# Cosine and sine tables of a state-space stage: two stored copies, or one copy that each load reads twice

## The chip, the core and the metric

The kernel runs on one core of a Trainium2 chip. The metric is the time of one execution on the device in microseconds (us); the kernel before was timed three times. One execution was also recorded by the hardware profiler, and all durations below are from that one.

## The reference, cut to what matters

Two layers work on 512 tokens of width 1024: chunked gated linear attention (GLA), then an S5 layer, each with an input projection, a gated branch of width 2048 and an output projection. The change is in the S5 layer. It runs 128 groups of 16 channels, each with 64 complex states:

```
lam_bar = jnp.exp(lam * dt)
bu = lax.complex(einsum(u, real(b_bar)), einsum(u, imag(b_bar)))
_, states = lax.associative_scan(combine, (a, bu), axis=1)      # state <- lam_bar * state + bu
y = einsum(real(states), c_re) - einsum(imag(states), c_im)
y = gelu(y + d_skip * u);  y = y * sigmoid(y @ w_glu + b_glu) * silu(z)
return y @ w_out
```

## The kernel before, in words

**Dense work.** All projections are products of 128x512 blocks on TensorE (PE). Weights come from HBM in units of 512 KB (`wunit`, L175, into one of two `wraw` buffers), and are split into a high and a low part on ScalarE (ACT, L158 or L180) and VectorE (DVE, L159) or by an accumulating DMA from GpSimd (POOL), into one of eight `whl` buffers. Each product is three matmuls (L189 to L195).

**The S5 recurrence.** The sequence is cut in 64 chunks of 8 tokens. Inside a chunk the recurrence is a small product; between chunks it is a scan on DVE with a real decay, which needs the states turned by an angle that depends on state, group and chunk before the scan and turned back after it. The turning uses tables of cosine and sine: for each of the 16 blocks (`cb`) of 8 groups, 512 values of each for each of the 64 states. Since real and imaginary parts of the states lie on partitions 0 to 63 and 64 to 127, the loaded table has to stand on both halves.

**Where the tables come from and go.** While the GLA layer runs, the class `S5Prep` prepares the S5 constants on DVE and stores them to scratch tensors in HBM: `bmd`, `cmd`, `gmd`, and the tables in `tab`. `etab(ck)` computes two blocks at once, on partitions 0 to 63 and 64 to 127 (six DVE instructions, L1251 to L1256), and stores each twice, to rows 0 to 63 and to rows 64 to 127 of its block (L1257 to L1260). Later `load_a(cb)` and `load_b(cb)` bring a block's four constants back through `loadw`: the first three blocks as two halves into `big` buffers (L569), the other 13 as one load of 512 KB into `q4` buffers (L572; the profile shows them as `q`). `sA` uses them: L795 to L798 are the first turn.

**What sets the order.** A scheduler with its own timing model orders the instructions of each engine when the kernel is built; `issue_after` and priorities steer it. Nearly all loads and stores are issued by SyncE (SP), in one order; an SP instruction that waits holds up those behind it. The `q4` tag has nine buffers, which the preparation, the blocks' constants and the gate outputs share, so that a load for a later block waits until an earlier block has been used. `F` steps of the preparation (L1267 to L1273) load `lpt` and `s_bi`, both with written-out patterns: `lpt` is read as 16 copies (step 0) of 8 rows, `s_bi` as 16 rows of 8 copies.

Of the kernel before, what the change touches and what calls it, by code (L numbers as in the profile page):

```python
# [9 lines left out]
F32 = mybir.dt.float32  # L10
# [11 lines left out]
P = 128  # L22
# [8 lines left out]
NS = 64  # L31
T = 8
NC = SEQ // T
GB = 8
NB = 16
# [52 lines left out]
def trunk_kernel(  # L88
# [5 lines left out]
    nc = tc.nc  # L94
# [3 lines left out]
    dr = ctx.enter_context(tc.tile_pool(name="dr", bufs=1, space=DRAM))  # L98
    cnt = [0]

    def T_(shape, tag, bufs, dt=F32):
        cnt[0] += 1
        return sb.tile(shape, dt, tag=tag, name=f"{tag}_{cnt[0]}", bufs=bufs)

    def C_(shape, name, dt=F32):
        return sb.tile(shape, dt, tag=name, name=name, bufs=1)
# [17 lines left out]
    def q4(dt=F32, n=1024):  # L124
        return T_([P, n], "q4", Q4, dt)
# [7 lines left out]
    def xx(dt=F32):  # L133
        return T_([P, 512], "xx", 8, dt)
# [189 lines left out]
    prep = S5Prep(tc, dr, C_, T_, PT, ident, q4, q2, big, tmp, s_bi, s_xc)  # L324
# [143 lines left out]
    for i in range(2):  # L468
        a = C_([P, P], f"att{i}")
# [87 lines left out]
    def loadw(cb, src, dt=F16):  # L557
        n = 1024 if dt == F16 else 512
        if src is prep.gmd:
            srcs = [src[cb, 4 * k:4 * k + 4].rearrange("g p w -> p g w") for k in range(2)]  # L560
            full = src[cb].rearrange("g p w -> p g w")
        else:
            srcs = [src[cb][:, k * n:(k + 1) * n] for k in range(2)]
            full = src[cb]
        fit = (lambda t: t.rearrange("p (g w) -> p g w", w=2 * P)) if src is prep.gmd else (lambda t: t)
        if cb < NPRE:
            w = [T_([P, n], "big", BIG, dt) for _ in range(2)]
            for k in range(2):
                S.dma_start(out=fit(w[k]), in_=srcs[k])  # L569
            return w  # L570
        t = q4(dt, 2 * n)
        S.dma_start(out=fit(t), in_=full)  # L572
        return [t[:, :n], t[:, n:]]
# [8 lines left out]
    def load_a(cb):  # L582
        t = st_[cb]
        t["bm"] = wsel(loadw(cb, prep.bmd))
        t["cs"] = loadw(cb, prep.tab, F32)

    def load_b(cb):
        t = st_[cb]
        t["gh"] = gsel(loadw(cb, prep.gmd))
        t["cm"] = wsel(loadw(cb, prep.cmd))  # L590
# [37 lines left out]
    for h in range(NH):  # L628
        v = ([], [])
        box = []  # L630
        o = ([], [])
# [64 lines left out]
    for i in range(2):  # L696
        r = xx().rearrange("p (g c) -> p g c", g=GB)
# [207 lines left out]
    for tb in range(NT):  # L905
        for k in range(2):
            S.dma_start(out=f(x1p)[k * 64:(k + 1) * 64, 2 * tb:2 * tb + 2].rearrange("p q d -> p (q d)"),
                        in_=x1d.rearrange("(c j) d -> j c d", j=T)[2 * tb + k])
# [21 lines left out]
class S5Prep:  # L930
    def __init__(self, tc, dr, C_, T_, PT, ident, q4, q2, big, tmp, s_bi, s_xc):
        self.tc = tc
        self.nc = nc = tc.nc
        self.C_, self.T_, self.PT, self.ident = C_, T_, PT, ident
        self.q4, self.q2, self.big, self.tmp = q4, q2, big, tmp
        self.s_bi, self.s_xc = s_bi, s_xc
        self.kz = dr.tile([NG, 16, KW * 2], F16, name="kz")
        self.bmd = dr.tile([NB, P, 2 * GB * P], F16, name="bmd")
        self.cmd = dr.tile([NB, P, 2 * GB * P], F16, name="cmd")
        self.gmd = dr.tile([NB, GB, P, 2 * P], F16, name="gmd")  # L940
        self.tab = dr.tile([NB, P, 2 * GB * NC], F32, name="tab")
        self.pw = dr.tile([2 * NS, NG, 2 * T], F32, name="pw")
        self.lpt = dr.tile([T, NG, 2, NS], F32, name="lpt")
        self.bcd = dr.tile([2, NS, NG], F32, name="bcd")
        self.r8d = dr.tile([NS, NG], F32, name="r8d")
        self.kdd = dr.tile([NG, 16], F32, name="kdd")
        self.etd = dr.tile([NG], F32, name="etd")
        self.t = 0
        self.ld = {}
        self.res = {}  # L950
# [290 lines left out]
    def etab(self, ck):  # L1241
        nc = self.nc
        tt = nc.vector.tensor_tensor
        gs = slice(ck * GB, (ck + 1) * GB)
        hr, hi, lr, li = (t[:, gs] for t in self.et)
        shp = [P, GB, 8, 8]
        up = lambda t: t.unsqueeze(3).to_broadcast(shp)
        dn = lambda t: t.unsqueeze(2).to_broadcast(shp)
        e = self.q4().rearrange("p (r g a b) -> p r g a b", r=2, g=GB, a=8)
        u = self.tmp().rearrange("p (g a b) -> p g a b", g=GB, a=8)  # L1250
        tt(out=e[:, 0], in0=up(hr), in1=dn(lr), op=MUL)  # L1251
        tt(out=u, in0=up(hi), in1=dn(li), op=MUL)
        tt(out=e[:, 0], in0=e[:, 0], in1=u, op=SUB)
        tt(out=e[:, 1], in0=up(hr), in1=dn(li), op=MUL)
        tt(out=u, in0=up(hi), in1=dn(lr), op=MUL)
        tt(out=e[:, 1], in0=e[:, 1], in1=u, op=ADD)  # L1256
        for k in range(2):  # L1257
            for r in range(2):
                nc.sync.dma_start(out=self.tab[k * 8 + ck, r * 64:(r + 1) * 64],
                                  in_=e[k * 64:(k + 1) * 64].rearrange("p r g a b -> p (r g a b)"))  # L1260

    def load(self, cb):
        S = self.nc.sync
# [155 lines left out]
```

## Time and profile before

| what | value |
|---|---|
| runs shown | 1040.68, 1044.32, 1048.78 us; median 1044.32 |
| profiled execution | 1042.2 us, of which the recorded span is 1040.5 us |
| mean granted clock of TensorE | 0.943 of full speed |
| busy share of the span | PE 89%, DVE 69%, ACT 45%, POOL 10% |
| moved by DMA | 205.79 MB; HBM read 167.69 MB, written 45.59 MB |

PE, DVE, ACT and POOL are the compute engines; SP only issues transfers. The page of the profile cuts the span into 40 slices and gives for each the busy tenths of an engine, the granted clock of PE and the mean busy share of the core's 16 DMA engines. Other views group instructions by line, list who waited for whom, list transfers with the time from issue to landing, or give the sums over a chosen stretch of the span.

### The profile page before, as it was taken

To read this page: it belongs to the slowest core of one execution; us is meant where nothing else is said; L and a number is where in the kernel's file an instruction comes from. 1 tells how busy PE (TensorE), PEld (TensorE's weight loads), DVE (VectorE), ACT (ScalarE), POOL (GpSimd) and SP (SyncE) were. 2 spreads that over 40 slices of the span, in tenths; PEclk is the share of its full clock that TensorE was granted. 3 is DMA by queue.
4 is the path that set the end of the run, shared out by engine and by line. 5 is a ranking of instruction groups with operands and counts; after the bars stand their busy time and mean duration, and the time that the engine had idled before them with its cause. 6 is when DMAs were issued, how large, how long until landed. Compare 5 with 4: busy or idle time off the path is not lost. (4 is left out here: it accounts for less than half of the span.)

```text
span 1040.5 us, 13590 instructions
## 1 busy us (share of the span) xinstructions
PE 921.3 (89%) x5019; PEld 715.9 (69%) x5019; DVE 715.5 (69%) x1225; ACT 471.4 (45%) x707; POOL 101.2 (10%) x168
## 2 busy tenths in 40 slices
PE   6895961899969984989999979999999999999996
PEld 5573750676747763767777768787778888888885
DVE  5793559977899768988947758798998542424322
ACT  5553342436546643543666573743443532313212
POOL 4175700002001200000100000000000000000000
PEclk9997985799979987999999989999999999999998
DMA  8884376899979999899684526777766432252312
GB/s 258 233 180 99 69 203 196 233 263 286 295 229 246 287 284 288 235 281 312 214 247 171 182 92 218 249 263 254 237 186 200 128 102 83 99 170 93 101 61 81
DMA packets 118707, 205.79 MB, mean 198 GB/s; under 512 B 32400, under 2 KB 69824, under 8 KB 118640
## 3 DMA queue, kind: packets, MB, share of 16 engines
q1 hardware_dynamic: 110208, 180.90, 54.9%
q0 software_dynamic: 5472, 19.02, 9.9%
q10 hardware_dynamic: 2960, 4.99, 1.4%
q8 instruction: 39, 0.64, 0.2%
q14 instruction: 28, 0.23, 0.1%
HBM read 167.69 MB, written 45.59 MB: 205 GB/s over the span
## 5 line engine op out<-in xcount | busy, mean ns | idle before, releaser
L159 DVE TENSOR_TENSOR whl<-wraw,whl 128x1024 fp32r<-128x1024 f32 x100 | 122.0, 1222 | 156.5 <-ACT whl L158 156.2
L158 ACT CAST whl<-wraw 128x1024 fp32r<-128x1024 f32 x100 | 104.9, 1049 | 191.1 <-PE pd L194 50.2
L193 PE MATMUL pd<-whl,actA 128*128 128x512 f32 x384 | 152.9, 404 | 13.3 <-ACT whl L158 9.0
L194 PE MATMUL pd<-whl,actA 128*128 128x512 f32 x384 | 153.0, 398 | 0.0
L195 PE MATMUL pd<-whl,actA 128*128 128x512 f32 x384 | 151.4, 399 | 0.0
L189 PE MATMUL pd<-actA,whl 128*128 128x512 f32 x256 | 102.3, 406 | 7.3 <-ACT u L723 6.2
L191 PE MATMUL pd<-actA,whl 128*128 128x512 f32 x256 | 101.4, 397 | 0.0
L193 PEld LDWEIGHTS pd<-whl,actA 128*128 128x128 f32 x384 | 73.1, 191 | 32.4 <-ACT whl L158 9.0
L195 PEld LDWEIGHTS pd<-whl,actA 128*128 128x128 f32 x384 | 72.9, 190 | 17.6 <-issue 2.4
L194 PEld LDWEIGHTS pd<-whl,actA 128*128 128x128 f32 x384 | 73.1, 190 | 16.9 <-issue 1.2
L193 PE MATMUL pd<-whl,q 128*128 128x512 f32 x192 | 79.0, 412 | 4.4 <-DVE tmp L387 2.7
L194 PE MATMUL pd<-whl,q 128*128 128x512 f32 x192 | 77.9, 406 | 0.0
L180 ACT CAST whl<-wraw 128x1024 fp32r<-128x1024 f32 x36 | 37.7, 1047 | 74.7 <-PE pd L194 32.2
L189 PEld LDWEIGHTS pd<-actA,whl 128*128 128x128 f32 x256 | 48.6, 190 | 19.8 <-ACT u L723 7.2
L191 PEld LDWEIGHTS pd<-actA,whl 128*128 128x128 f32 x256 | 48.7, 190 | 11.3
L189 PE MATMUL po<-actA,whl 128*128 128x512 f32 x128 | 51.7, 404 | 3.8 <-ACT whl L180 3.8
L190 PE MATMUL pd<-actA,whl 128*128 128x512 f32 x128 | 52.1, 407 | 0.0
L191 PE MATMUL po<-actA,whl 128*128 128x512 f32 x128 | 50.4, 396 | 1.3 <-DMA whl<-w_qk 1.3
L195 PE MATMUL pd<-whl,q 128*128 128x512 f32 x128 | 50.9, 409 | 0.0
L723 ACT ACTIVATE u<-pd,rsP 64x256 f32<-64x256 f32 x64 | 48.2, 753 | 3.5 <-DVE mxr L716 2.6
L190 PE MATMUL pd<-big,whl 128*128 128x512 f32 x120 | 47.6, 398 | 1.1 <-DVE big L159 1.1
L193 PEld LDWEIGHTS pd<-whl,q 128*128 128x128 f32 x192 | 37.3, 194 | 15.4 <-DVE tmp L387 3.1
(327 smaller groups left out, 2001.2 us busy)
## 6 DMA issues: line engine op xcount, KB each, us to landing
wraw<-w_glu SPq DMA_DIRECT2D x32, 512.0 KB, 3.5
wraw<-w_v SPq DMA_DIRECT2D x16, 512.0 KB, 4.7
wraw<-w_z SPq DMA_DIRECT2D x16, 512.0 KB, 6.7
whl<-w_z POOLq DMA_DIRECT2D x16, 512.0 KB, 7.9
q<-lpt SPq DMA_DIRECT2D x16, 512.0 KB, 6.8
q<-s_bi SPq DMA_DIRECT2D x16, 512.0 KB, 8.5
wraw<-w_out SPq DMA_DIRECT2D x16, 512.0 KB, 5.5
bmd<-q SPq DMA_DIRECT2D x16, 512.0 KB, 5.1
```

The costliest lines, as they stand in the source:

```text
L158: i0 = A.copy(out=dst_hi, in_=src)
L159: i1 = V.tensor_tensor(out=dst_lo, in0=src, in1=f(dst_hi), op=SUB)
L180: A.copy(out=hi, in_=raw)
L189: PE.matmul(acc, lhsT=wh, rhs=ah, start=first, stop=False)
L190: PE.matmul(acc, lhsT=wh, rhs=al, start=False, stop=False)
L191: mark["pe"] = PE.matmul(acc, lhsT=wl, rhs=ah, start=False, stop=last).ins
L193: PE.matmul(acc, lhsT=ah, rhs=wh, start=first, stop=False)
L194: PE.matmul(acc, lhsT=ah, rhs=wl, start=False, stop=False)
L195: mark["pe"] = PE.matmul(acc, lhsT=al, rhs=wh, start=False, stop=last).ins
L723: A.activation(out=dst, in_=src, func=AF.Copy, scale=rsP[hs, tb:tb + 1])
```

## The change

`tab` gets 64 rows for each block in place of 128. `etab` stores each block once: two stores of 256 KB for a call in place of four, so 16 in the program in place of 32. `loadw` reads the 64 rows twice, by a pattern whose first count is 2 with step 0, then 64 rows, then the run of the row. The tile that a load fills, and its size, stay as they are.

```diff
+        if src is prep.tab:
+            w2 = 2 * GB * NC
+            both = lambda o, m: bass.AP(src.tensor, src[cb].offset + o, [[0, 2], [w2, NS], [1, m]])
+            srcs, full = [both(k * n, n) for k in range(2)], both(0, w2)
         fit = (lambda t: t.rearrange("p (g w) -> p g w", w=2 * P)) if src is prep.gmd else (lambda t: t)
...
-        self.tab = dr.tile([NB, P, 2 * GB * NC], F32, name="tab")
+        self.tab = dr.tile([NB, NS, 2 * GB * NC], F32, name="tab")
...
         for k in range(2):
-            for r in range(2):
-                nc.sync.dma_start(out=self.tab[k * 8 + ck, r * 64:(r + 1) * 64],
-                                  in_=e[k * 64:(k + 1) * 64].rearrange("p r g a b -> p (r g a b)"))
+            nc.sync.dma_start(out=self.tab[k * 8 + ck], in_=e[k * 64:(k + 1) * 64].rearrange("p r g a b -> p (r g a b)"))
```

The scheduler places everything anew. The first place is SP's queue at the first two calls of `etab`; each row is an instruction with its target, its source and its size. Before:

```order
L1259 DMA tab<-q_232_1282 64x1024 x4
L1272 DMA big_1408<-s_xc 128x512
L1259 DMA tab<-q_241_1343 64x1024 x2
L1273 DMA pp_1409<-pw 128x128
L1259 DMA tab<-q_241_1343 64x1024 x2
L1309 DMA cmd<-q_261_1451 128x2048
L1309 DMA bmd<-q_305_1646 128x2048
L1267 DMA q_311_1665<-lpt 128x1x1024
```

In the changed program, whose lines behind `loadw` are numbered 4 and behind `etab` 2 higher:

```order
L1262 DMA tab<-q_232_1282 64x1024 x2
L1274 DMA big_1404<-s_xc 128x512
L1262 DMA tab<-q_241_1341 64x1024 x2
L1311 DMA cmd<-q_261_1447 128x2048
L1275 DMA pp_1405<-pw 128x128
L1311 DMA bmd<-q_305_1640 128x2048
L1269 DMA q_311_1659<-lpt 128x1x1024
```

Four of eight stores are gone, and `cmd` stands one place ahead of `pp`. The second place is SP's queue where the third block's halves are loaded, at the end of the GLA layer. In the changed program:

```order
L175 DMA wraw_4130<-w_out 128x1024
L175 DMA wraw_4170<-w_out 128x1024
L573 DMA big_4209<-bmd 128x1024
L573 DMA big_4210<-bmd 128x1024
L1342 DMA gmd<-kz 1024x1x256
L573 DMA big_4213<-tab 128x1x512
L1337 DMA kz<-kf_3738 128x256
L573 DMA big_4214<-tab 128x1x512
L573 DMA big_4217<-gmd 128x4x256
L175 DMA wraw_4296<-s_wu 128x1024
```

Before, the copy `gmd<-kz` stood between the two `tab` halves instead of ahead of both, and their rows read `tab 128x512`. The third place is the main S5 stage; in the changed program:

```order
L576 DMA q_1017_5252<-bmd 128x2048
L576 DMA q_1018_5254<-tab 128x1x1024
L576 DMA q_1019_5256<-gmd 128x8x256
L576 DMA q_1020_5258<-cmd 128x2048
L175 DMA wraw_5267<-s_wz 128x1024
```

From here on SP's order is the same as before, load by load. Only the form of the `tab` row differs, `128x1x1024` for `128x1024`: the source now has counts of its own (2, 64, 1024), as the `lpt` row of the first place has.

## Rows read from the trace of the kernel before

**Rows 1.** The page: busy us of each engine, and its DMA row.

```profile
PE 921.3 (89%) x5019; PEld 715.9 (69%) x5019; DVE 715.5 (69%) x1225; ACT 471.4 (45%) x707; POOL 101.2 (10%) x168
DMA  8884376899979999899684526777766432252312
```

**Rows 2.** Stretches: start:end, us, busy us by engine, granted clock, DMA share, GB/s.

```profile
176.00:220.00 44.00, 35.03 (x139) 26.63 (x138) 41.05 (x71) 20.89 (x32) 2.63 (x3) 0.79 0.85 232
300.00:400.00 100.00, 95.84 (x414) 73.86 (x410) 82.33 (x142) 54.55 (x80) 10.67 (x11) 0.95 1.00 280
400.00:420.00 20.00, 6.50 (x31) 3.85 (x31) 17.62 (x40) 9.82 (x18) 1.73 (x2) 0.57 0.92 249
456.00:480.00 24.00, 21.29 (x85) 14.95 (x84) 22.47 (x48) 8.66 (x18) 1.03 (x1) 0.93 0.98 325
480.00:510.00 30.00, 28.45 (x135) 21.28 (x133) 25.69 (x46) 14.82 (x30) 0.00 (x0) 1.00 0.66 226
543.00:630.00 87.00, 78.81 (x646) 62.45 (x646) 56.21 (x92) 55.49 (x74) 0.34 (x2) 0.96 0.46 152
630.00:752.00 122.00, 119.83 (x1079) 95.95 (x1078) 106.95 (x154) 58.39 (x83) 1.90 (x11) 1.00 0.75 249
```

**Rows 3.** DMA issues: count, KB of each, median us from issue to landing.

```profile
q<-lpt SPq DMA_DIRECT2D x16, 512.0 KB, 6.8
q<-s_bi SPq DMA_DIRECT2D x16, 512.0 KB, 8.5
...
wraw<-s_wu SPq DMA_DIRECT2D x16, 512.0 KB, 3.5
...
q<-tab SPq DMA_DIRECT2D x13, 512.0 KB, 6.5
```

**Rows 4.** SP's time for one issue, ns minimum/median/maximum, by line.

```profile
L1259 SPq DMA_DIRECT2D tab<-q x32: 452/654/1544, 177.7 to 539.0; - x32
L572 SPq DMA_DIRECT2D q<-tab x13: 319/383/660, 543.3 to 752.5; - x13
L1267 SPq DMA_DIRECT2D q<-lpt x16: 520/530/1324, 144.9 to 440.5; - x16
```

**Rows 5.** Waits that DVE (300 to 400 us) and PE (400 to 500 us) ended.

```profile
DVE q L1283 <- DMA q<-s_bi: 10.3, 3, 4.7
...
PE pt L1323 <- DVE q L162: 7.5, 1, 7.5
PE pt L1323 <- DVE big L159: 5.7, 1, 5.7
```

**Rows 6.** SP in order of time: start, us, line.

```profile
363.75 2.77 SPq L1259 DMA_DIRECT2D tab<-q  x4
...
474.81 0.55 SPq L1340 DMA_DIRECT2D gmd<-kz  x1
...
481.10 0.33 SPq L175 DMA_DIRECT2D wraw<-s_wu  x1
```

**Rows 7.** ACT in order of time: the split of the first `s_wu` unit.

```profile
494.62 1.05 ACT L158 CAST whl<-wraw 128x1024 fp32r<-128x1024 f32 x1 [3.62 <-PE pd L194]
```

**Rows 8.** DMA from 630 to 752 us: GB/s in 40 slices, then `tab` loads.

```profile
GB/s 305 363 259 364 208 0 198 336 361 309 103 335 380 167 60 0 174 361 409 334 105 216 363 374 248 115 340 357 365 39 156 349 376 316 15 0 244 258 330 348
...
q<-tab SPq DMA_DIRECT2D x9, 512.0 KB, 6.5
```

**Rows 9.** SP in order of time: two `tab` loads of that stretch.

```profile
647.86 0.32 SPq L572 DMA_DIRECT2D q<-tab  x1
...
665.67 0.51 SPq L572 DMA_DIRECT2D q<-tab  x1
```

**Rows 10.** DVE: the first uses of these two tables.

```profile
667.22 0.69 DVE L795 TENSOR_TENSOR tmp<-po,q 64x512 f32<-64x512 f32 x1
...
701.39 0.69 DVE L795 TENSOR_TENSOR tmp<-po,q 64x512 f32<-64x512 f32 x1
```

**Rows 11.** Waits of SP's queue, 540 to 770 us.

```profile
SPq L572 <- PE pt L765: 54.2, 13, 9.9
```

## The prediction

> **What bounds the kernel now.** I read the page first [rows 1]. PE is busy 921.3 of 1040.5 us, and no other engine is near it, so a gain can come only where PE waits, or where something that it needs comes late. The DMA row has digits of 8 and 9 in its first fifteen and then around slice 19, and 5 to 7 afterwards: transfers are a near-bound in the GLA layer, where the preparation runs, and have room later. Then I took stretches [rows 2]. The reader is to see three things there. From 300 to 400 us the 16 DMA engines are full (share 1.00, 280 GB/s) while PE still gets 95.8 of 100 us. From 400 to 420 us PE works only 6.5 of 20 us, and its granted clock falls to 0.57. And from 630 to 752 us PE is full (119.8 of 122 us) with a DMA share of 0.75. The waits [rows 5] say why PE stands at 400: its small matmuls of the preparation (L1323) wait 7.5 and 5.7 us for DVE, which shortly before had waited 10.3 us for the `s_bi` loads. So transfers are paid for there by way of DVE, and behind 630 us they are hidden, as long as they come in time.
>
> **The stores.** Sixteen of 32 stores of 256 KB go. On SP each takes a median of 0.654 us [rows 4], 10.5 us in all; SP is no compute engine, and what counts is what it issues behind them. Half belong to the first four calls of `etab`, of which the first starts at 177.7 us [rows 4] and the fourth at 363.75 [rows 6]; the other half belong to the last four, the last of them at 539.0 [rows 4]. A call saves 0.5 MB, or 1.9 us of full DMA at the 280 GB/s of 300 to 400 us [rows 2]. Two of these calls lie in the full stretch and two ahead of it, where DVE is the busiest (41.05 of 44 us from 176 to 220) and the DMA share is 0.85. The last four lie where PE loses little (28.45 of 30 us busy from 480 to 510), so I count them as nothing; their cover is PE's own work, and without it they save another 7.5. The gain lies between 0 and 4 x 1.9 = 7.5 us; I take 3, since only part of DVE's waiting reaches PE.
>
> **The order.** Some matmuls of the preparation change places by a few rows, `cmd` goes ahead of `pp`, and `gmd<-kz` goes ahead of a `tab` load. Nothing is added to an engine. What this costs isn't in the trace; it can go either way, and the nearest row is the 13.2 us of stall that PE has behind L1323 [rows 5], as a whole given back or had once more. I take 0, and keep 5 us on each side, because the rows that move stay within a few places.
>
> **The loads, issue.** A load of `tab` becomes a source with written-out counts, like `lpt`, whose issue takes 0.530 us against 0.383 [rows 4]: 19 loads, 2.8 us of SP. In the S5 stage SP waits 54.2 us for buffers that PE has still to free [rows 11], which covers it; without that cover it is 2.8 us.
>
> **The loads, on the engines.** This is the term that decides. Before, a load is 128 rows, spread evenly over 16 engines: 8 rows each. Now its pattern is 2 x 64 rows, with steps of 0 and 1024 elements, which don't merge into one count. How such a pattern is spread isn't shown by any row. At one end it is spread as before, at no cost. At the other, the first count decides, and two engines carry 64 rows each. The nearest rows are `lpt` and `s_bi` [rows 3], the other loads with two counts: they land in 6.8 and 8.5 us, near the 6.5 of the flat load, but their first count is 16, so both readings fit them. What is new is the 2, and I take the end at which it counts: a flat 128, or a 16 in front, is what all large loads here have in common. I further take it that it is the same two engines each time.
>
> [...]
>
> *From 630 to 752 us.* A share of 0.75 at 249 GB/s [rows 2] is 249 / 0.75 / 16 = 20.75 GB/s for a busy engine, or 0.197 us for a row of 4 KB; the fastest slice, 409 GB/s [rows 8], is 25.6 GB/s, or 0.160 us. An engine is busy 0.75 x 122 = 91.5 us. Nine `tab` loads [rows 8] are 72 rows of that, 14.2 us (11.5 at the fast price), and other transfers 77.3 (80.0). With 64 rows a load, two engines get 576 rows, 113.5 (92.2) us, together 190.8 (172.2) us in a stretch of 122: 69 (50) us too much. Every other load has a share on these two engines and lands no sooner than they do, weights included. What absorbs some of it is the lead of the loads. Two of them [rows 9] are first used 19.4 and 35.7 us after their issue [rows 10]; less the 6.5 us of landing, 12.9 and 29.2, on average 21. That leaves 48 (29) us; I take 38. The bounds are 0, if leads grow by themselves, and 69. From 543 to 630 us three loads add 3 x 56 x 0.197 = 33 us to 0.46 x 87 = 40 us, which fits into 87: nothing there.
>
> *From 456 to 510 us.* Six loads of 256 KB, rows of 2 KB: two engines get 336 rows or 688 KB more, 33 us at 20.75 GB/s, 27 at 25.6, in a stretch with a share of 0.98 [rows 2]. From 480 to 510 us 0.34 x 30 = 10.2 us are free for it. Queued behind are the store of `kz` and the copy `gmd<-kz` that waits for it at 474.81 us, and behind that in SP's order the first `s_wu` unit at 481.10 [rows 6]. That unit lands after 3.5 us [rows 3] and is split at 494.62 [rows 7], so it has 10 us to spare. 27 to 33, less 10.2, less 10, are 7 to 13 us of PE standing; I take 10, with bounds of 0 and 33.
>
> **The sum.** -3 + 0 + 0 + 38 + 10 = +45 us on the profiled execution of 1042.2 us. The median of the runs is 1044.3, 2.1 above, so I predict 1089 us. With the longer lead, the fast price, no loss before 510 us and the full gain of the stores it is 50 - 29 - 7.5 = +13.5, or 1058; with the shorter lead, the slow price and the full 33 us it is 69 - 13 + 33 = +89, or 1133. That is the range of this case.
>
> **Rivals.**
> *Sixteen engines as before.* The two counts are spread over all engines. For it speaks that `lpt` and `s_bi`, with two counts, pay nothing; against it that theirs begin with 16. Then only the stores are left: 1044.3 - 3 = 1041 us, not slower. It decides at the stall at 400 us, behind the third and fourth call: to be faster by over 1%, most of its 13.2 us [rows 5] have to go, where two stores' worth of DMA is 1.9 us a call. It shows by `tab` loads that still land in under 8.5 us.
> *Two engines, but other ones each time.* Then each load takes 64 x 0.160 to 0.197 = 10 to 13 us in place of 6.5, within the smallest lead of 12.9 beyond landing, and no engine is full for long: 1041 to 1050, say 1044. Against it: nothing in the trace shows a rotation.
> *Two engines, and no lead helps.* The loads of the next block start only when PE has freed buffers [rows 11], so a late load delays the next one's start, and PE's clock falls in its pauses, as at 400 us [rows 2]: up to 1044.3 + 69 + 33 = 1146, say 1140.
>
> **Chances.** A measurement of this kernel tells about 1%, 10 us, from no change. The forecast gets 0.70, since no other large load has a first count that leaves engines out and the excess of 50 to 69 us is twice the lead; 0.04 of it ends within 1%, the rest slower. Sixteen engines get 0.17, of which 0.05 faster and 0.12 the same; rotation 0.08, of which 0.07 the same and 0.01 slower; no lead 0.05, slower. Together: faster 0.05, same 0.23, slower 0.72. The range of 1040 to 1132 leaves out half of the sixteen-engine case (0.085), the last rival (0.05) and the forecast's upper tail (some 0.05).
>
> **What would show it.** Right: the median landing of `q<-tab` rises above 10 us; the DMA share falls while the S5 stage grows; waits of DVE's L795 for `q<-tab`, and of ACT's L158 for `wraw`, appear; PE's idle time grows behind 456 us and hardly before. HBM written falls by 4.2 MB in any case. Wrong: `q<-tab` lands in 5 to 8 us (sixteen engines), or in 10 to 13 us with PE as full as before (rotation); or PE loses its time ahead of 456 us, which would be the order.

## The result, and the profile after

The changed kernel takes 1132.7 us (median of 4 runs, 1128.1 to 1135.7) against 1043.0 us for the kernel before (four runs), a ratio of 1.085 with an interval of 1.082 to 1.089. The profiled execution took 1128.1 us (span 1126.4) against 1042.2, so 85.9 us have to be found. The numbers of lines behind `loadw` are four higher in the changed kernel (L576 for L572, L836 for L832).

The page of the changed kernel, PE's busy row, the DMA row by slices and the first part of the chain of waits [rows 1]:

```profile
PE 945.8 (84%) x5019; PEld 730.8 (65%) x5019; DVE 714.8 (63%) x1225; ACT 470.0 (42%) x707; POOL 99.8 (9%) x168
...
DMA  8864466999789988648645356464566432244222
...
PE 46%; DMA 25%; DVE 15%; ACT 6%; issue 4%; SPq 2%; POOL 0%; ACTq 0%; DVEq 0%; POOLq 0%
```

PE runs the same 5019 matmuls in 24.5 us more, and stands the other 61 us. The DMA digits go down in the middle of the program, not up, though what is loaded is the same. The same stretches as in [rows 2]:

```profile
300.00:400.00 100.00, 96.10 (x399) 72.47 (x400) 81.71 (x141) 51.12 (x76) 10.69 (x11) 0.96 0.96 265
...
456.00:480.00 24.00, 18.67 (x74) 13.90 (x73) 22.01 (x42) 7.15 (x11) 1.03 (x1) 0.86 0.61 210
480.00:510.00 30.00, 21.23 (x68) 15.05 (x68) 14.02 (x28) 7.17 (x16) 0.00 (x0) 0.72 0.51 166
630.00:752.00 122.00, 101.57 (x825) 80.98 (x826) 70.22 (x106) 54.99 (x78) 1.03 (x6) 0.89 0.49 152
```

From 300 to 400 us nothing has changed that matters. From 456 us on PE's busy time falls, its granted clock with it (1.00 to 0.72 from 480 to 510 us), and the DMA share drops from 0.98 to 0.61 and from 0.75 to 0.49. Engines that stand while others have a queue would look like this.

Fixed times compare different work, so I cut both traces at the same loads: the first, the seventh (the first of 512 KB), the tenth and the last `tab` load. Before, these were issued at 455.88, 543.30, 629.88 and 752.45 us; after, at 461.41, 564.43, 659.14 and 836.09. Columns as in [rows 2]; first the kernel before:

```profile
455.88:543.30 87.42, 81.67 (x379) 61.93 (x378) 68.98 (x129) 43.93 (x78) 4.06 (x7) 0.98 0.81 261
543.30:629.88 86.58, 78.39 (x643) 62.08 (x642) 55.95 (x91) 55.20 (x74) 0.34 (x2) 0.96 0.46 152
629.88:752.45 122.57, 120.16 (x1080) 96.16 (x1080) 107.51 (x154) 58.84 (x84) 1.90 (x11) 1.00 0.75 249
```

and the changed kernel:

```profile
461.41:564.43 103.02, 86.15 (x373) 65.15 (x372) 67.54 (x127) 43.20 (x77) 4.06 (x7) 0.88 0.62 202
564.43:659.14 94.71, 79.57 (x643) 63.20 (x642) 56.13 (x91) 55.06 (x74) 0.34 (x2) 0.91 0.45 138
659.14:836.09 176.95, 130.99 (x1080) 103.70 (x1080) 107.02 (x153) 56.81 (x82) 1.89 (x11) 0.87 0.58 176
```

Ahead of the first load the program is 5.5 us later. The three stretches grow by 15.6, 8.1 and 54.4 us, and what follows by 2.3: together 85.9. In the last stretch the matmuls are the same 1080; 43.6 of the 54.4 us are PE standing, and 10.8 are the same matmuls at a granted clock of 0.87 in place of 1.00.

The medians from issue to landing [rows 3]; the table loads have none in this trace:

```profile
wraw<-s_wz SPq DMA_DIRECT2D x16, 512.0 KB, 14.8
...
q<-gmd SPq DMA_DIRECT2D x13, 512.0 KB, 10.9
...
xx<-yd SPq DMA_DIRECT2D x16, 256.0 KB, 8.0
```

Weights of `s_wz` landed in 5.9 us before, `gmd` in 6.5, `xx<-yd` (y coming back through HBM) in 4.2. What is late is the flat loads beside the table loads. SP's time for one issue, ns minimum/median/maximum, as in [rows 4]:

```profile
L576 SPq DMA_DIRECT2D q<-tab x13: 512/512/781, 564.4 to 836.1; - x13
L576 SPq DMA_DIRECT2D q<-gmd x13: 370/436/10653, 577.1 to 860.9; - x13
L576 SPq DMA_DIRECT2D q<-cmd x13: 319/1817/10721, 581.7 to 862.4; - x13
```

Before, the longest issue of these lines was 2.8 us (`cmd`). Now SP is held for up to 10.7 us in a single issue. One round in the S5 stage, from the timeline of the changed kernel (start, duration, engine; in brackets the idle time before and what ended it), shows how that reaches PE:

```profile
676.50 0.38 SPq L175 DMA_DIRECT2D wraw<-s_wz  x1
677.11 0.51 SPq L576 DMA_DIRECT2D q<-tab  x1
677.67 1.08 SPq L831 DMA_DIRECT2D xx<-yd  x1
679.19 10.65 SPq L576 DMA_DIRECT2D q<-gmd  x1
689.93 4.25 SPq L576 DMA_DIRECT2D q<-cmd  x1
...
695.49 0.72 ACT L836 ACTIVATE big<-xx,mx 128x512 f32<-128x512 f32 x1 [10.72 <-DMA xx<-yd]
699.71 1.04 ACT L158 CAST whl<-wraw 128x1024 fp32r<-128x1024 f32 x1 [3.50 <-DMA wraw<-s_wz]
700.66 2.91 ACT L727 ACTIVATE u<-pd,rsP 64x256 f32<-64x256 f32 x4
...
703.62 0.79 PE L189 MATMUL pd<-actA,whl 128*128 128x512 f32 x1 [10.47 <-ACT u L727]
```

The load of `xx` leaves SP half a microsecond behind a table load. ACT gets its data 18 us later, and its evictions of `u` are queued behind that, and PE stands 10.5 us for `u`. Before, from 543 us to 24 us behind the last `tab` load (776 us), ACT waited 3.3 us for `xx<-yd` and 10.4 for `s_wz`; in the changed kernel, over the same work (543 to 860 us):

```profile
ACT whl L158 <- DMA wraw<-s_wz: 56.4, 7, 14.9
ACT big L836 <- DMA xx<-yd: 23.4, 7, 10.7
```

### The profile page after: what moved, and what is told of

Same layout as the page of the kernel before. It is cut to its first block, busy times and chain, and to the rows that moved or that the text cites. A ratio compares the mean times of both kernels' runs of the same rounds, so it can differ in the third digit from the quotient of the medians.

```text
span 1126.4 us, 13569 instructions
## 1 busy us (share of the span) xinstructions
PE 945.8 (84%) x5019; PEld 730.8 (65%) x5019; DVE 714.8 (63%) x1225; ACT 470.0 (42%) x707; POOL 99.8 (9%) x168
## 4 chain that ended last, share of the span: by engine, by line
PE 46%; DMA 25%; DVE 15%; ACT 6%; issue 4%; SPq 2%; POOL 0%; ACTq 0%; DVEq 0%; POOLq 0%
DMA wraw<-s_wz 7%; PE pd L193 6%; PE pd L194 6%; PE pd L195 6%; DMA big<-s_xc 4%; PE pd L190 4%; PE pd L189 4%; PE pd L191 4%; ACT u L727 3%; DMA wraw<-w_v 2%; DMA q<-s_bi 2%; DVE whl L159 2%; PE po L189 2%; PE po L190 2%; PE po L191 2%
## 5 line engine op out<-in xcount | busy, mean ns | idle before, releaser
L189 PE MATMUL pd<-actA,whl 128*128 128x512 f32 x256 | 107.2, 426 | 40.1 <-ACT u L727 20.8
L191 PE MATMUL pd<-actA,whl 128*128 128x512 f32 x256 | 105.3, 412 | 0.0
L193 PE MATMUL pd<-whl,q 128*128 128x512 f32 x192 | 81.3, 425 | 18.1 <-DVE tmp L387 8.2
L189 PEld LDWEIGHTS pd<-actA,whl 128*128 128x128 f32 x256 | 51.4, 201 | 54.2 <-ACT u L727 21.7
L194 PE MATMUL pd<-whl,q 128*128 128x512 f32 x192 | 80.6, 420 | 0.0
L191 PEld LDWEIGHTS pd<-actA,whl 128*128 128x128 f32 x256 | 51.3, 200 | 12.2
L180 ACT CAST whl<-wraw 128x1024 fp32r<-128x1024 f32 x36 | 37.7, 1046 | 47.6 <-PE pd L194 21.5
L195 PE MATMUL pd<-whl,q 128*128 128x512 f32 x128 | 54.4, 433 | 1.6 <-DVE q L162 1.6
L190 PE MATMUL pd<-actA,whl 128*128 128x512 f32 x128 | 55.5, 433 | 0.0
```

Source lines behind the costliest of these rows:

```text
L180: A.copy(out=hi, in_=raw)
L189: PE.matmul(acc, lhsT=wh, rhs=ah, start=first, stop=False)
L190: PE.matmul(acc, lhsT=wh, rhs=al, start=False, stop=False)
L191: mark["pe"] = PE.matmul(acc, lhsT=wl, rhs=ah, start=False, stop=last).ins
L193: PE.matmul(acc, lhsT=ah, rhs=wh, start=first, stop=False)
L194: PE.matmul(acc, lhsT=ah, rhs=wl, start=False, stop=False)
```

## The experiments

**Form, repetition or order.** Theory A: the first count of 2 puts each table load on two engines, the same each time. Theory B: the stores and the new order cost. Theory D: reading rows again costs, on however many engines. The first run (e1) is the kernel before with only the pattern of the load (32 stores, PE's and DVE's instructions in the order of before):

```diff
+        if src is prep.tab:
+            w2 = 2 * GB * NC
+            both = lambda o, m: bass.AP(src.tensor, src[cb].offset + o, [[0, 2], [w2, 64], [1, m]])
+            srcs, full = [both(k * n, n) for k in range(2)], both(0, w2)
```

> The kernel before with its 32 stores, its order on PE and on DVE; only the 19 loads of the tables read rows 0 to 63 of a block by the pattern 2 (step 0) x 64. Theory A (the first count of 2 puts a load on two of 16 DMA engines): all of the loss, 1125 to 1145 us. Theory B (the new order of the changed kernel costs): 1043 us, plus or minus 5. Theory C (stores and loads share it): in between, near 1090.

Measured: 1126.2 us, ratio 1.079 (1.075 to 1.082). The form alone carries 83 of the 90 us. The second (e2) is the changed kernel, its stores and its 64 rows, but each load in two flat ones:

```diff
-        both = lambda o, m: bass.AP(src.tensor, src[cb].offset + o, [[0, 2], [w2, NS], [1, m]])
...
+            for r in range(2):
+                S.dma_start(out=t[r * 64:(r + 1) * 64], in_=src[cb])
```

> The changed kernel (64 stored rows, 16 stores) with each table load written as two loads of 64 flat rows, one for each half of the partitions. Theory A: back to the time before, less the stores, 1035 to 1046 us. Theory B (order): stays above 1100, since the order is near that of the changed kernel. Theory D (reading the same 64 rows of HBM twice is what costs): stays above 1100 too.

Measured: 1051.45 us, 1.007 (1.004 to 1.010): the loss is gone, but the time is above the 1035 to 1046 that I expected. The third (e3) is the first with `[[0, 16], [w2, 8], [1, m]]`: 8 rows, read sixteen times.

> The kernel before with the table loads read by the pattern 16 (step 0) x 8, so that a load takes 8 rows 16 times; the tables are then not the right ones, which changes no time. Theory A: 1043 us, plus or minus 5, as all 16 engines share a load. Theory D (re-reading, or the form with written-out counts): above 1100, since eight rows are read 16 times.

Measured: 1048.5 us, 1.005 (1.003 to 1.007). Rows read again cost next to nothing when the first count is 16. Theory D falls, and B is left with under 1%.

**What one load does.** Loads of 512 KB alone (e4). `S` issues on SP and `A` on ACT's queue; behind it stands the first count, where `P`, 128, is the flat load:

```diff
+    for first in (P, 16, 8, 4, 2, P, 16, 8, 4, 2):
+        phase([(S, first)])
+    for _ in range(2):
+        phase([(S, 2), (S, 2)])
+        phase([(S, 2), (S, P)])
+        phase([(S, 2), (A, P)])
...
```

> Not the layer: only loads of 512 KB, each phase by itself, and adds that read them. Ten single loads (first count 128, 16, 8, 4, 2, twice over), then twice: two loads with first count 2; one with 2 and a flat one; one with 2 on SP and a flat one on ACT's queue; five flat ones; one with 2 and four flat ones. Theory A: 128 and 16 land in 3 to 5 us, 8 in about 5, 4 in 7 to 8, 2 in 11 to 14. If the two engines are the same each time, the second of two such loads lands 10 us after the first, and a flat load behind one lands with it, in over 10 us, from SP and from ACT's queue; if they change, both land at once and the flat one in 4 to 6 us. Theory D: 16 is as slow as 2.

The timeline of this run: a load with first count 2, a flat one, then two with a 2 (`a`, `b`), each issue and its first reader:

```profile
42.72 0.52 SPq L36 DMA_DIRECT2D a<-w  x1
55.36 1.04 ACT L42 COPY cp<-a 128x1024 f32<-128x1024 f32 x1 [16.14 <-DMA a<-w]
59.90 0.34 SPq L36 DMA_DIRECT2D a<-w  x1
63.70 1.04 ACT L42 COPY cp<-a 128x1024 f32<-128x1024 f32 x1 [7.29 <-DMA a<-w]
...
118.38 0.52 SPq L36 DMA_DIRECT2D a<-w  x1
118.95 0.51 SPq L36 DMA_DIRECT2D b<-w  x1
130.42 1.04 ACT L42 COPY cp<-a 128x1024 f32<-128x1024 f32 x1 [15.55 <-DMA a<-w]
140.40 1.23 DVE L40 TENSOR_TENSOR end<-end,b 128x1024 f32<-128x1024 f32 x1 [19.68 <-DMA b<-w]
```

Flat took 3.8 us, and first counts of 16, 8, 4 and 2 took 4.8, 6.5, 8.5 and 12.6. From 45 to 54 us, inside a 2, this row of the stretches stands (DVE, ACT and POOL, clock, DMA share, GB/s):

```profile
45.00:54.00 9.00, 0.07 (x1) 0.00 (x0) 0.00 (x0) 1.00 0.13 53
```

A share of 0.13 is two engines of sixteen, and 53 / 0.13 / 16 = 25.5 GB/s for one, 0.161 us for a row of 4 KB. The second of two such loads comes 10.0 us behind the first: they share their engines. A flat load behind a 2 on SP came after 13.1 us, from ACT's queue after 7.0.

**Where the loss arises.** The form for the six loads of 256 KB only (e5, `cb < NPRE`), and for the 13 of 512 KB only (e6, `cb >= NPRE`):

```diff
-        if src is prep.tab:
+        if src is prep.tab and cb < NPRE:
```

> The kernel before, with the repeating pattern (counts 2, 64) only for the six loads of 256 KB of the first three blocks; the 13 loads of 512 KB stay flat. Theory A (two engines carry each such load, and what they lose in a stretch is kept): the run with the form alone lost 17 us between its first table load and the first one of 512 KB, so 1043 + 17 = 1060 us (1053 to 1064), and 17 us again between those two loads in the trace. Rival (the loss grows out of one place and is only carried on: the late start of the S5 stage is what makes all later loads late): most of the 83 us appear already, above 1090 us. Rival (the six loads cost nothing, all of the loss belongs to the 13): 1043 to 1046 us.

Measured: 1059.8 us against 1044.5, 1.014 (1.010 to 1.018): +15.3.

> The kernel before, with the repeating pattern only for the 13 loads of 512 KB; the six of 256 KB stay flat. Theory A: the run with the form alone lost 63 us between the first and the last of these loads, so 1043 + 63 = 1106 us (1098 to 1112), and with the run of the first blocks the two losses add up to that of the form alone (83 us). Rival (one place carries all): 1043 to 1060 us. My prediction's term for this stretch was 38 us, 1081.

Measured: 1108.4 us, 1.061 (1.056 to 1.065): +63.9. The sum of 79.2 is nearly the 83.4 of the form alone. Cut at the same loads as above, e5 grows by 16.7 us from the first to the seventh load and by nothing in the two stretches behind; e6 grows by nothing, 7.2 and 55.6. The losses arise in their own stretches and are not given back.

**The table loads from another queue.** The form, with the 13 loads issued by POOL (e7), and a control with flat loads from POOL (e8):

```diff
-        S.dma_start(out=fit(t), in_=full)
+        (nc.gpsimd if src is prep.tab else S).dma_start(out=fit(t), in_=full)
```

> The form alone on the kernel before, but all 13 loads of 512 KB are issued by POOL and not by SP. In the changed kernel SP was held for up to 10.7 us in issuing a load behind a table load. Theory Q (what costs is the queue: what stands behind a table load in SP's queue is held with it, so the loss of 63 us comes from that queue): SP is held no more, its issues take under 3 us at most, and the loss of the S5 stage falls to a third or less, 1043 + 17 + up to 20 = 1060 to 1080 us. Theory C (what costs is the capacity of two engines, whoever issues): 576 rows more in a stretch of 122 us stay 50 to 69 us too much, 1110 to 1130 us. If POOL's transfers are spread over other engines, or over all: 1060 us, the loss of the first blocks alone.

> Control for the run with the loads on POOL: the kernel before, flat table loads, the 13 loads of 512 KB issued by POOL. Both theories: within 1% of the kernel before, 1035 to 1053 us; if POOL's issue itself costs (it runs beside DVE's work), the excess over 1043 has to be taken off the run with the pattern.

Measured: 1107.2 us, 1.060 (1.056 to 1.064), and 1043.05, 0.998 (0.995 to 1.000). The control is free. With 15 us for the six loads on SP, about 47 are left where the 13 on SP cost 64: the time is just under theory C's 1110 to 1130 and far over theory Q's 1060 to 1080. The table loads landed after a median of 18.2 us here, `gmd` after 15.3 and `xx<-yd` after 13.3. SP was still held, but less: 3.2 us at most for `gmd` in place of 10.7, 5.0 for `s_wz` in place of 9.2, with one `bmd` of 10.5. So SP's queue alone doesn't carry the loss.

**Four engines.** The form with `[[0, 4], [w2, 32], [1, m]]` (e9):

> The form alone with a first count of 4 (32 rows, each read four times; the tables are wrong by that, which changes no time). Theory A (the first count is the number of engines): four engines get 32 rows a load in place of 8. In the S5 stage that is 9 x 24 = 216 rows more, 42.6 us at 0.197, on 91.5 us in a stretch of 122: 134 us, 12 too much (5 at the fast price of 0.160), and the lead of 21 us covers it, so the stage costs 0 to 5 us; the six early loads put 6 x 24 rows of 2 KB, 14 us, on four engines, and 0 to 5 us of that stay. 1044 to 1056 us, near the 1048 of the first count 16. Rival (any load that reads its rows again on part of the engines costs by its own landing time, so in proportion to it): loads alone took 3.8, 8.5 and 12.6 us with first counts of 128, 4 and 2, which gives 82 x (8.5 - 3.8) / (12.6 - 3.8) = 44 us, 1088 us.

Measured: 1083.1 us (1074.1 to 1089.2), 1.034 (1.026 to 1.042). My working for theory A misses by 27 us; the rival, in proportion to landing times, comes within 5. The last nine loads in this trace, as cut above:

```profile
646.80:795.96 149.16, 126.66 (x1080) 100.68 (x1080) 107.09 (x153) 56.88 (x82) 1.88 (x11) 0.93 0.75 207
```

The stretch is 26.6 us longer than before; I had counted 134 us of work for a loaded engine and got 149. What I had held fixed is the cost of the other transfers. An estimate from the rows, with 0.161 us for a table row and all else spread evenly: before, an engine is busy 0.75 x 122.57 = 91.9 us, of which 72 rows are 11.6, so 80.3 are other work. Here it is 0.75 x 149.16 = 111.9 on average, 100.3 without the table, and a loaded engine has 100.3 + 288 x 0.161 = 146.7 of 149.2 us. In the changed kernel it has 0.58 x 176.95 - 11.6 + 576 x 0.161 = 183.8 of 177. By this estimate the loaded engines are full in both, and the same other bytes take 10 to 20 us longer. The records don't give the share by engine, so it stays an estimate.

The trace of the changed kernel can be asked whether it fits. Its GB/s in 40 slices, from 659.14 to 836.09 us; [rows 8] has the row before:

```profile
GB/s 342 192 99 62 320 179 53 144 314 193 232 56 149 163 189 51 235 320 161 186 54 256 201 105 156 188 168 128 74 223 29 247 333 64 148 245 235 177 56 296
```

Where [rows 8] goes down to 0, seven of the nine lowest slices here stand at 51 to 64, near the 53 of two engines alone in e4. The single DMA packets have a start and a duration in the trace, though no engine, so I counted how many are in flight at once. Inside the 2 of e4, from 45 to 54 us, two are for 95% of the time and never fewer. In this stretch at least two are for 97% of the time, and just two or three for 40% of it; before, 79% and 3%. With a first count of 4, at least four are for 94%. So in both runs the loaded engines can have had little time to spare.

**What the stores are worth.** The kernel before, 32 stores, with each load in two flat halves of 64 rows (e10):

```diff
+        parts = [slice(0, 64), slice(64, P)] if src is prep.tab else [slice(0, P)]
...
+        for r in parts:
+            S.dma_start(out=fit(t[r]), in_=full[r])
```

> The kernel before, both copies stored (32 stores), but each table load in two flat halves of 64 rows, as in the run with two loads, which stored one copy (16 stores). It tells what the saved stores are worth. My prediction's term: the stores saved are 3 us (0 to 7.5), so this kernel is 3 us slower than that run, 1054 us (1051 to 1059). Rival (the stores are worth nothing or the new order costs): 1044 to 1051 us, at or below the 1051.5 of that run.

Measured: 1048.6 us, 1.003 (1.001 to 1.006), beside the 1.007 (1.004 to 1.010) of the second run. The 16 stores that were saved, together with the order that came with them, give nothing that can be measured. The two are not parted: a small gain from the stores could be hidden by a cost of the order. Stores alone, with the loads and the order as before, were not tried.

**Which queues share.** Loads alone again (e11), from SP, ACT and POOL (`G`), and a row of five as in the S5 stage ("s" is 1024 rows of 512 B, as `gmd` has):

```diff
...
+        phase([(S, 2), (G, 2)])
...
+        phase([(S, 2), (A, 2)])
+        phase([(S, P), (S, 2), (S, "s"), (S, P), (S, P)])
+        phase([(S, P), (S, P), (S, "s"), (S, P), (S, P)])
...
```

> Loads of 512 KB alone, from SP, ACT and POOL, with the time from issue to the first reader; no part of the reference is computed. Alone on SP a first count of 2 took 12.6 us, two of them on SP came in 10 us apart. Theory C (the two engines are the same whichever engine issues): 2 on SP and 2 on POOL at once end at 12.6 and 22 us, or both near 22. Rival (POOL's transfers go to other engines): both end at 12 to 14 us. On SP and ACT at once: the same two cases. Then flat, first count 2, 1024 rows of 512 B, and two flat loads in a row on SP, as in the S5 stage: if the queue of each engine holds few rows, SP is held for up to 10 us in issuing the third, fourth or fifth; with a flat load in place of the 2, or with the 2 on POOL, it is not held (issues under 1.5 us).

The timeline, the pair on SP and POOL, the pair on SP and ACT, then the row of five as SP issues it:

```profile
27.75 0.69 SPq L38 DMA_DIRECT2D a<-w  x1
28.57 1.29 POOL L38 DMA_DIRECT2D b<-w  x1 [16.91 <-DVE b L52]
40.00 1.04 ACT L44 COPY cp<-a 128x1024 f32<-128x1024 f32 x1 [15.76 <-DMA a<-w]
42.39 1.23 DVE L42 TENSOR_TENSOR end<-end,b 128x1024 f32<-128x1024 f32 x1 [12.04 <-DMA b<-w]
...
69.31 0.50 SPq L38 DMA_DIRECT2D a<-w  x1
69.88 1.11 ACTq L38 DMA_DIRECT2D b<-w  x1
88.78 1.04 ACT L44 COPY cp<-a 128x1024 f32<-128x1024 f32 x1 [24.31 <-DMA a<-w]
91.61 1.23 DVE L42 TENSOR_TENSOR end<-end,b 128x1024 f32<-128x1024 f32 x1 [19.96 <-DMA b<-w]
...
99.30 0.53 SPq L38 DMA_DIRECT2D b<-w  x1
99.90 0.45 SPq L38 DMA_DIRECT2D c<-w  x1
100.50 8.67 SPq L38 DMA_DIRECT2D d<-w  x1
```

SP and ACT share the two engines (19.5 and 21.7 us); POOL's load goes beside SP's (12.3 and 13.8), so POOL's are others. The DMA share inside the two pairs says the same: 0.27 of sixteen is four engines for SP and POOL, 0.13 two for SP and ACT (columns as in e4):

```profile
30.00:39.00 9.00, 0.35 (x1) 0.00 (x0) 0.00 (x0) 1.00 0.27 94
73.00:88.00 15.00, 0.00 (x0) 0.00 (x0) 0.00 (x0) 1.00 0.13 53
```

Which engines these are, and whether POOL's change from load to load, no run here shows. With the 2 in the row, SP is held 8.67 us at the fourth load; with a flat load in its place, or with the 2 on POOL, no issue of SP took over 0.63 us.

**Weights out of the queue.** The form, with the `s_wz` units issued by POOL (e12; theory W: these weights, right behind table loads in SP's queue, are the cost):

```diff
-        mark["sp"] = S.dma_start(out=raw.rearrange("p k n -> p (k n)"), in_=src).ins
+        on_q = G if src.tensor is s_wz.tensor else S
+        mark["sp"] = on_q.dma_start(out=raw.rearrange("p k n -> p (k n)"), in_=src).ins
```

> The form alone on the kernel before (all 19 table loads with counts 2, 64, on SP), but the 16 weight units of s_wz, which stand behind table loads in SP's queue, are issued by POOL. The scheduler moves some other instructions with that, so only a large step tells something. Theory W (each table load delays what stands behind it in SP's queue, and weight units with two buffers have no lead; a flat load behind a first count of 2 came after 13.1 us on the same queue and 8.3 from POOL): in the run with the form alone ACT waited 57.9 us for s_wz; that falls below 25 us and the time to 1085 to 1105 us. Theory C (two engines are over their capacity in the S5 stage, and every load has its share on them, from whichever queue): 1118 to 1130 us, as with the form alone, and ACT's waits for s_wz stay above 45 us.

Measured: 1122.4 us, 1.073 (1.070 to 1.077). ACT's waits from 543 to 860 us in this run:

```profile
ACT big L837 <- DMA xx<-yd: 69.5, 9, 15.9
...
ACT whl L158 <- DMA wraw<-s_wz: 1.4, 1, 1.4
```

The waits for `s_wz` are gone, as theory W said, and the time is not: ACT now waits 69.5 us for `xx<-yd`, which still stands behind table loads on SP. The weights were only where the lateness showed. Theory W falls.

## Why the prediction was right, and where its sizes were off

The forecast had the cause and the direction, and about half of the size: +45 us on the profiled execution, where 85.9 were measured. The median of 1132.7 us lies at the upper end of my range (1132) and nearer to the rival without a lead (1140) than to my 1089.

**The loads, on the engines.** Right, and shown: the first count decides (1.079 with a 2 in e1 and 1.005 with a 16 in e3; 12.6 us and 4.8 alone in e4), and two loads from SP have the same engines (the pair in e4, 10.0 us apart). The rivals with sixteen engines as before and with a rotation are out.

**From 630 to 752 us: +54.4, predicted 38.** This is the term that was mis-sized. My sum gave a loaded engine 172 to 191 us of work in a stretch of 122, and the stretch became 177. The step that failed is the lead of 21 us that I took off. It belonged to the table loads, and these do have it: no wait of DVE's L795 (L799 in the changed kernel) for `q<-tab` appears. The shortest time from the issue of such a load of 512 KB to its first use is 23.5 us, well over the 12.6 that it takes alone:

```profile
702.46 0.51 SPq L576 DMA_DIRECT2D q<-tab  x1
...
725.96 0.69 DVE L799 TENSOR_TENSOR tmp<-po,q 64x512 f32<-64x512 f32 x1
```

But late are the flat loads that share the two engines, `xx<-yd` and `s_wz`, and they have no such lead. I had written that every other load lands no sooner than the two engines do, and then used the wrong load's lead. The price of the rival without a lead for this stretch, 69, is too high by about as much as my 38 is too low; with no lead and the fast price of 0.160 for a row, which e4 confirms (0.161), my own sum gives 50. My sum also had no term for PE's clock in its pauses, 10.8 us of PE's time in the 54.4; I named that only in that rival. Whether these 10.8 us lengthen the stretch isn't shown: as long as the loaded engines are full, a faster PE would only stand longer.

**From 543 to 630 us: +8.1, predicted 0.** The work fitted on average (33 + 40 of 87 us), and e6 puts the loss on the loads of 512 KB (+7.2). An average over a stretch can hide loads that arrive together; that this is the reason isn't shown.

**From 456 to 510 us: +10, measured +15.6 from the first to the seventh load, +15.3 by e5.** Inside my bounds of 0 and 33. PE stands as said, from 480 to 510 us for 8.8 us against 1.6 before; 4.5 of the 15.6 are more busy time, for fewer matmuls at a granted clock of 0.88 in place of 0.98, a term that was missing here too.

**The stores and the order: -3 and 0 predicted, nothing seen.** HBM written fell by 4.2 MB as it must, to 41.4. The first `tab` load is 5.5 us later in the profile, but e10 against e2 puts the stores and the order together within 1%. The nine other runs of the whole kernel that keep the 32 stores stand between 2.3 us earlier and 6.4 later at that point, so 5.5 is within what one profile scatters; e2, 10.4 us later, is outside of it, so a small cost of the order isn't excluded. I had also misplaced the calls: the third starts at 215.84 us, so only the fourth lies in the full stretch from 300 to 400, and the last four start at 509.74, behind the stretch that I quoted for them. And the first fifteen digits of the DMA row [rows 1] aren't all 8 and 9: five of them are 3 to 7. The sum doesn't change by it.

**The issue.** 0.512 us against 0.383 [rows 4], as said. What I did not see is that a load behind can hold SP up to 10.7 us. I had costed SP's time at 2.8 us and covered it by waits for buffers [rows 11].

**The signs to look for.** The DMA share fell while the stage grew, ACT's waits for `wraw` appeared, PE lost its time behind 456 us: all there. L795's wait was not, as told. The landing of `q<-tab` has no row in this trace; the loads alone give 12.6 us, and e7, from POOL, 18.2.

What stays open is how the loss divides between the two engines being full and the order in SP's queue. Two and four engines on SP fit the first, by the estimate and by the packets in flight, and e12 moved the wait from one transfer to another without changing the time. The 47 us of e7 don't fit it well: from 658.92 to 805.59 us, its last nine table loads, just two or three packets are in flight for only 7% of the time, four to six for 18% and none for 6% (3%, 5% and 15% in e8's last nine), which points to several pairs of engines and to none that is full. There the table loads and the flat loads beside them are late all the same, and no run isolates why. No run tried here beats the kernel before: the nearest that stores one copy, two flat loads (e2), costs 0.7%.

## What to carry to other kernels

Read the first count of a transfer's pattern before its bytes: the same 512 KB took 3.8 us flat and 12.6 us with a leading 2, and in this kernel the repeated read cost 0.7% as two flat loads (e2), 8.5% with the 2. When some DMA engines get much more than the others, add up what the fullest engine has to do, and take off only the lead of the loads that share it with the least lead, not that of the transfer which causes it. A wait that is removed at one transfer (e12) proves nothing until the time falls.

## What was not expected of the hardware

SP was held in issuing: up to 10.7 us in the changed kernel, 8.67 us with the loads alone (e11), there at the fourth load. By an estimate from the patterns, with a flat load even over sixteen engines (before, from 544 to 547 us, inside flat loads, the DMA share is 0.95) and one with a 2 on two (0.13 in e4), one engine's rows issued up to and with that load are 8 + 64 + 64 + 8 = 144, and 8 + 8 + 64 + 8 + 8 = 96 in the row of e11 that was not held (0.63 us at most); in e4's row of a 2 and four flat loads, also 96, no issue took over 0.53 us. Whether the rows per engine are what counts, no run varied by itself.
